# A hybrid pooling, spatial-gating and mLSTM layer: the gating projection in one pass of 512 columns, its weights split on VectorE, its rows normalised on ScalarE

## The chip, the cores and the metric

The kernel runs on one core of a Trainium2 chip. The metric is the device time of one execution in microseconds (us). The engines are named as the profile names them: PE is TensorE (PEld its weight loads), DVE is VectorE, ACT is ScalarE, POOL is GpSimd, SP is SyncE, which here only issues DMAs.

## The reference, cut to what matters

One layer works on 256 context tokens and 1024 latent tokens with the same weights. The part that the change touches is the input projection of the spatial branch's `v` half and the normalisation of its rows:

```python
u = rmsnorm(x, g_norm1) * (1 + sc1) + sh1
proj = u @ w_in
xp, su, sv, q, k, v, o_pre, gate_pre, br_pre = jnp.split(proj, points, axis=-1)
y_a = pool_branch(xp, w_pool, pool_scale, grid)
y_b = sgu_branch(su, sv, g_sgu, w_sgu, b_sgu)      # 512 columns each
y_c, C_out, n_out, m_out = mlstm_branch(q, k, v, o_pre, ...)

def sgu_branch(u, v, g_sgu, w_sgu, b_sgu):
    vn = rmsnorm(v, g_sgu).reshape(B, T // CHUNK, CHUNK, N_SGU_GROUPS, SGU_GROUP)
    mixed = jnp.einsum('gpq,bnqgc->bnpgc', w_sgu, vn) + ...
    return u * mixed.reshape(B, T, D_SGU)
```

All of it is float32. The three branches are gated, summed and projected (`w_out`), and a feed-forward follows with 4096 hidden columns.

## The kernel before, in words

The 1280 tokens are ten tiles of 128 (NT = 10), or three token groups of 512, 512 and 256 columns. The contraction over the model's 1024 features is eight steps of 128 (KT = 8). A float32 product is made of three matmuls on rounded halves: high by high, low by high and high by low. Weights arrive by DMA as `raw` tiles of 128x1024, two at a time (NRAW = 2). `load_w` (L88 to L95) makes the high half with a cast on ACT (L93) and the low half with a subtraction on an engine that the caller names (L94). There are three buffers for each half (NHL = 3). Activations and results live in 59 buffers of 128x512, called slots (L55), which are given out again once the last reader of a slot is done.

In PSUM there are three banks for large products (`ps_mm`) and five for smaller ones (`ps_sd`). A bank is free again when the last instruction that reads it is done.

The order of the instructions on each engine is not the order of the source, outside a pinned prologue. A scheduler that simulates the program puts the instructions of all engines into an order when the program is built; on the chip each engine takes its own row strictly in that order, and waits at the first instruction whose inputs or whose buffer are not ready. A change in one place can therefore move work elsewhere.

The part around the change runs from about 273 to 421 us. Two heads of the mLSTM branch (the third and the fourth, whose tiles carry the head's number 2 and 3) and the projections for them and for the pooling branch (`p_xp`) are interleaved with the `sv` matmuls, which are independent of the heads and fill PE between their steps. One head does the following. `tk` and `tv` transpose keys and values on PE (L582, L586); ACT copies them out (L583, L587), DVE scales them (L590). `kv` (L597) are 18 matmuls that DVE adds one after the other into a running state (L608, L613). `st` and `rb` (L626, L630) give the weights of a group, made ready on DVE and ACT (L634 to L644). `pv` (L659, L661) gives the outputs of a tile. From there a chain of small steps goes through ACT, DVE and POOL: L664, L665, L666, L667, L668, L669, L129, L130 (the power -0.5, on POOL) and L673 (rows scaled, on ACT); then `th` transposes the result on PE (L674) and ACT copies it out (L676, `yc`).

The `sv` part itself (L697 to L716) goes twice over the ten token tiles, each time with 256 of the 512 weight columns. Per tile it runs 24 matmuls of 256 columns into one bank (L707 to L709), ACT copies the bank to the slot `vn` (L710) and squares it with a sum over the row (L711). Each pass loads its own two weight tiles, the low halves on POOL. After the second pass the two sums of a row are added on DVE (L713), `rstd_of` makes the reciprocal root (L129 on DVE, L130 on POOL), and DVE scales the ten tiles (L716). The scaled rows are the stationary side of the `mx` matmuls in `spatial` (L840), whose results DVE takes (`mt`, L844) and multiplies with the projection `p_su` (L851). The pooling branch works beside it on DVE and POOL (L767).

Of the kernel before, what the change touches and what calls it, by code (L numbers as in the profile page):

```python
# [7 lines left out]
F32 = mybir.dt.float32  # L8
F32R = mybir.dt.float32r
AF = mybir.ActivationFunctionType  # L10
ALU = mybir.AluOpType
# [3 lines left out]
P = 128  # L15
D = 1024
KT = D // P
NSAMP = 1024
T = 1280
NT = T // P  # L20
# [8 lines left out]
NTMP, NRAW, NHL = 5, 2, 3  # L29
# [19 lines left out]
def hybrid_step(  # L49
# [8 lines left out]
    V, A, G, PE = engines  # L58
# [6 lines left out]
    wp = pw.enter_context(tc.tile_pool(name="wp", bufs=NRAW))  # L65
# [3 lines left out]
    def slot(name, dt=F32R):  # L69
        return sp.tile([P, 512], dt, tag="s", name=name)  # L70
# [4 lines left out]
    def ps_mm(name):  # L75
        return pp.tile([P, 512], F32, tag="mm", name=name, bufs=3)
# [4 lines left out]
    def small(shape, name, bufs=4):  # L81
        return cp.tile(shape, F32, tag=f"sm{shape[-1]}", name=name, bufs=bufs)
# [6 lines left out]
    def load_w(src, name, raw=None, eng=V):  # L89
        raw = fetch_w(src, name) if raw is None else raw  # L90
        hi = wp.tile([P, 1024], F32R, tag="hi", name=f"hi_{name}", bufs=NHL)
        lo = wp.tile([P, 1024], F32R, tag="lo", name=f"lo_{name}", bufs=NHL)
        A.copy(hi, raw)  # L93
        eng.tensor_tensor(lo, raw, hi.bitcast(F32), ALU.subtract)  # L94
        return hi, lo  # L95
# [125 lines left out]
    uT = [[] for _ in range(KT)]  # L221
# [54 lines left out]
    V, A, G, PE = (Pinned(tc, e) for e in engines)  # L276
# [119 lines left out]
    for at, (g, k) in enumerate(steps):  # L396
# [3 lines left out]
        if (g, k) == (1, 2):  # L400
# [4 lines left out]
            for i in range(2):  # L405
                w = slot(f"wgs{i}").rearrange("p (k c) -> p k c", c=P)
# [25 lines left out]
    V, A, G, PE = engines  # L432
# [84 lines left out]
    for g in range(3):  # L517
        t0, n = GROUPS[g]
        r = slot(f"rhl{g}")
# [173 lines left out]

    vn = []
    vsq = cp.tile([P, NT, 2], F32, name="vsq")
    for q in range(2):
        wq = [load_w(w_sv[q, hf], f"sv{q}_{hf}", eng=G) for hf in range(2)]  # L697
        for i in range(NT):
            g, o = (i * P) // 512, (i * P) % 512
            if q == 0:  # L700
                vn.append(slot(f"vn{i}", F32))
            ps = ps_mm(f"sv{q}_{i}")
            for k in range(KT):
                whi, wlo = wq[k // 4]
                s = slice((k % 4) * 256, (k % 4 + 1) * 256)
                uh, ul = uT[k][g]
                PE.matmul(ps[:, :256], uh[:, o : o + P], whi[:, s], start=k == 0, stop=False)  # L707
                PE.matmul(ps[:, :256], ul[:, o : o + P], whi[:, s], start=False, stop=False)
                PE.matmul(ps[:, :256], uh[:, o : o + P], wlo[:, s], start=False, stop=k == KT - 1)  # L709
            A.copy(vn[i][:, q * 256 : (q + 1) * 256], ps[:, :256])  # L710
            A.activation(ps[:, 256:512], ps[:, :256], AF.Square, accum_out=vsq[:, i, q : q + 1])  # L711
    vs1 = small([P, 16], "vs1")[:, :NT]
    V.reduce_sum(vs1, vsq, axis=mybir.AxisListType.X)  # L713
    r = rstd_of(vs1, NT, "v")
    for i in range(NT):
        V.tensor_scalar(vn[i], vn[i], r[:, i : i + 1], None, ALU.mult)  # L716

    def zs(i, n=1):
        return z[:, i * 512 : (i + n) * 512]
# [336 lines left out]
    for ri, r in enumerate(ORDER):  # L1056
        scr = (scr_ya, scr_yb, scr_yc)[r]
        ys = [[] for _ in range(4)]
        for g in range(3):
            for kc in range(4):  # L1060
                t0, n = GROUPS[g]
                raw = tmp2(f"yr{r}_{kc}_{g}")
# [407 lines left out]
def _layout(inputs):  # L1470
    import numpy as np

    f = {k: np.asarray(v) for k, v in inputs.items()}
    a = {}
    a["xs"] = np.concatenate([f["x_sample"][0], f["x_prompt"][0]], 0).reshape(NT, P, D)

    def col(v, n):
        return v.reshape(n, P).T

    cond = np.stack([f["c"][0], f["c_ctx"]], -1).reshape(KT, P, 2).transpose(1, 0, 2).reshape(P, 16)  # L1480
    a["cols"] = np.concatenate(
        [
            cond, col(f["b_ada"][0, :2048], 16), col(f["g_norm1"][0], 8), col(f["g_norm2"][0], 8),
            col(f["pool_scale"][0], 4), col(f["g_sgu"][0], 4), col(f["g_mlstm"][0], 4),
        ], 1)
    s = np.arange(P)
    neg = np.float32(-1e30)
    a["consts"] = np.concatenate(
        [
            np.eye(P, dtype=np.float32),  # L1490
            np.where(s[:, None] <= s[None, :], np.float32(0), neg),
            np.where(s[:, None] >= s[None, :], np.float32(0), neg),
            np.tile(np.eye(2, dtype=np.float32), (64, 1)),
        ], 1).astype(np.float32)
    sel = np.zeros((100, 8), np.float32)
    for d in range(2):
        for h in range(H):
            sel[32 * d + h, 4 * d + h] = 1.0
            sel[64 + 32 * d + h, 4 * d + h] = 1.0
    a["sel8"] = sel  # L1500
    a["w_ada"] = f["w_ada"][0]
    a["b_ada"] = f["b_ada"]
    w = f["w_in"][0]
    wd = np.concatenate([w[:, :1024], w[:, 1536:3584], w[:, 3600:]], 1)
    a["w_in"] = wd.reshape(KT, P, 48, P).transpose(2, 1, 0, 3).reshape(48, P, KT * P)
    a["w_sv"] = w[:, 1024:1536].reshape(2, 4, P, 2, 256).transpose(3, 0, 2, 1, 4).reshape(2, 2, P, 1024)
    wgt = np.zeros((KT, P, P), np.float32)
    wk = w[:, 3584:3600].reshape(KT, P, 16)
    bg = np.zeros((36, 2), np.float32)
    m0 = np.zeros((36, 1), np.float32)  # L1510
    for t in range(2):
        for d in range(2):
            j = t * 8 + d * 4
            for o in (0, 4):
                wgt[:, :, 64 * t + 32 * d + o : 64 * t + 32 * d + o + 4] = wk[:, :, j : j + 4]
            bg[32 * d : 32 * d + 4, t] = f["b_gates"][0, j : j + 4]
    for d in range(2):
        m0[32 * d : 32 * d + 4, 0] = f["state_m"][0, 0, d]
    a["w_gate"] = wgt.transpose(1, 0, 2)
    a["bg"], a["m0"] = bg, m0  # L1520
    a["w_branch"] = f["w_branch"][0].reshape(3, 4, P, 4, 256).transpose(0, 3, 2, 1, 4).reshape(3, 4, P, 1024)
    a["w_out"] = f["w_out"][0].reshape(KT, P, 2, 512).transpose(2, 0, 1, 3)
    a["w_ff1"] = f["w_ff1"][0].reshape(KT, P, NFF, P).transpose(2, 1, 0, 3).reshape(NFF, P, D)
    a["w_ff2"] = f["w_ff2"][0].reshape(NFF, P, D)
    a["w_pool"] = f["w_pool"][0].transpose(1, 0, 2)
    a["w_sgu"] = f["w_sgu"][0].transpose(2, 0, 1)
    a["b_sgu"] = f["b_sgu"][0].reshape(1, 4 * P)

    def inv(n, win):
        t = np.arange(n)  # L1530
        cnt = np.clip(t + win - win // 2, 0, n) - np.clip(t - win // 2, 0, n)
        return (np.float32(1.0) / cnt.astype(np.float32)).astype(np.float32)

    a["pcnt"] = np.stack([
        np.concatenate([np.outer(inv(GRID_H, w_), inv(GRID_W, w_)).ravel(), inv(256, w_)]) for w_ in POOL_WINDOWS])
    st = np.concatenate([f["state_C"][0, 0], f["state_n"][0, 0][..., None]], -1)
    a["state"] = st.transpose(1, 2, 0, 3)
    a["gfin"] = f["g_final"].reshape(1, D)
    return {k: np.ascontiguousarray(v) for k, v in a.items()}
# [31 lines left out]
```

## Time and profile before

| what | value |
|---|---|
| time, median of 3 runs (lowest, highest) | 1940.14 us (1939.9, 1941.92) |
| the profiled execution's own time | 1940.92 us |
| its span in the profile | 1939.1 us |
| mean granted PE clock | 0.996 |
| PE busy / DVE / ACT / POOL | 98% / 67% / 44% / 19% |
| first `sv` matmul, first `p_su` matmul | 273.31 us, 420.66 us |

The median belongs to the timed runs, the rows of the profile to one execution of its own, which took 0.78 us longer than the median. A matmul's duration in the rows includes its filling and draining, which the next one overlaps; the pace of PE is therefore the distance between the starts of successive rows. A number in brackets at a row's end is the idle time of the engine before that instruction, with what ended it.

### The profile page before, as it was taken

The page shows a single profiled execution, that of the slowest core. Times are in us where ns is not written, and L with a number is a line of the kernel's source. Part 1 is how long each engine was busy: PE and PEld are TensorE (multiplying, and loading weights), DVE is VectorE, ACT ScalarE, POOL GpSimd, SP SyncE. Part 2 cuts the span into 40 slices and gives each one's busy share as a digit, 9 for nine tenths or more (in the row PEclk, how much of TensorE's full clock was granted, in tenths as well). Part 3 has the DMA queues.
Part 4 walks back from the last instruction along what each step waited for, and adds up shares of the span by engine and source line. Part 5 has one row for each costly group of instructions (what it writes and reads, how often), then busy time and mean ns, then how long its engine had stood idle before and what let it go on. Part 6 is the DMA issues. An engine that isn't in the chain of part 4 may idle for free.

```text
span 1939.1 us, 28222 instructions
## 1 busy us (share of the span) xinstructions
PE 1904.2 (98%) x10142; PEld 1628.1 (84%) x10142; DVE 1306.1 (67%) x2234; ACT 848.7 (44%) x1771; POOL 376.6 (19%) x381
## 2 busy tenths in 40 slices
PE   8989999999999999999999999999999999999998
PEld 5878898988888888888888887888888888888886
DVE  6575435578597878876665598887776655744665
ACT  6444455532433333342113375554454544443343
POOL 1100011064032422220000015544431210000003
PEclk9999999999999999999999999999999999999999
DMA  9211111025353434469622435777774686655544
GB/s 367 80 60 32 46 39 39 33 82 201 126 181 131 148 131 156 143 222 341 198 77 100 162 109 214 267 256 269 255 248 141 202 323 201 213 170 151 158 140 160
DMA packets 152774, 318.56 MB, mean 164 GB/s; under 512 B 17934, under 2 KB 42226, under 8 KB 150586
## 3 DMA queue, kind: packets, MB, share of 16 engines
q1 hardware_dynamic: 109082, 223.35, 35.1%
q0 software_dynamic: 15520, 57.75, 8.0%
q10 hardware_dynamic: 28032, 35.67, 5.1%
q8 instruction: 79, 1.29, 0.3%
q14 instruction: 61, 0.50, 0.1%
HBM read 220.21 MB, written 95.98 MB: 163 GB/s over the span
## 4 chain that ended last, share of the span: by engine, by line
PE 86%; DVE 5%; DMA 4%; ACT 2%; POOL 2%; issue 1%; SPq 0%; POOLq 0%; ACTq 0%; DVEq 0%
PE w L1438 6%; PE w L1439 6%; PE w L1440 6%; PE pb L1086 3%; PE pb L1085 3%; PE pb L1087 3%; PE fT_g L921 3%; PE fT_g L919 3%; PE fT_g L920 3%; PE fT L919 3%; PE fT L920 3%; PE fT L921 3%; PE fB L921 2%; PE fB L920 2%; PE fB L919 2%; PE fB_g L921 2%
## 5 line engine op out<-in xcount | busy, mean ns | idle before, releaser
L1277 POOL TENSOR_TENSOR z<-z 128x512 f32<-128x512 f32 x64 | 100.6, 1571 | 120.7 <-DMA z<-in_w_ff 117.7
L547 POOL PARTITION_ALL_REDUCE acc<-acc x16 | 54.5, 3441 | 226.5 <-DVE acc L541 123.0
L976 DVE TENSOR_TENSOR z<-z 128x512 f32<-128x512 f32 x120 | 94.9, 791 | 2.7
L541 DVE SCALAR_TENSOR_TENSOR acc<-z,scond,acc 128x512 f32<-128x512 f32 x112 | 82.3, 781 | 0.0
L1392 POOL TENSOR_TENSOR rs_y<-rs_y,neghalf 128x1 f32<-128x1 f32 x10 | 9.6, 966 | 332.8 <-DVE rs_y L1391 332.8
L1243 ACT ACTIVATE z<-z 128x512 f32<-128x512 f32 x64 | 40.5, 632 | 70.6 <-DVE z L985 35.6
L1002 ACT ACTIVATE z<-z 128x512 f32<-128x512 f32 x56 | 35.4, 632 | 65.3 <-DVE z L985 17.7
L130 POOL TENSOR_TENSOR rs_h<-rs_h,neghalf 128x4 f32<-128x4 f32 (+1 forms) x12 | 10.9, 910 | 178.8 <-DVE rs_h L129 144.0
L1091 DVE TENSOR_TENSOR sg<-pb,sg 128x512 f32<-128x512 f32 (+1 forms) x48 | 28.7, 601 | 24.0 <-PE pb L1087 23.9
L1244 ACT ACTIVATE z<-z 128x512 f32<-128x512 f32 x64 | 40.3, 629 | 1.1
L910 ACT CAST hi_wb<-raw_wb 128x512 fp32r<-128x512 f32 x24 | 14.8, 620 | 57.2 <-PE pb L1086 44.6
L1206 DVE TENSOR_TENSOR po<-po,gt 128x512 f32<-128x512 f32 (+1 forms) x24 | 14.6, 609 | 35.4 <-PE po L1205 35.3
L767 POOL TENSOR_TENSOR z<-z 128x256 f32<-128x256 f32 (+13 forms) x20 | 34.7, 1745 | 13.7 <-ACT z L752 5.5
L1268 POOL DMA_DIRECT2D scr_s<-x x48 | 26.3, 548 | 52.9 <-DVE x L1262 47.2
L548 POOL TENSOR_TENSOR acc<-acc,bt 1x512 f32<-1x512 f32 x16 | 22.3, 1408 | 60.0 <-issue 60.0
L1209 ACT ACTIVATE po<-z 128x512 f32<-128x512 f32 (+1 forms) x24 | 12.7, 529 | 48.3 <-DVE z L1208 34.0
L608 DVE SCALAR_TENSOR_TENSOR z<-z,dmb,kv 128x129 f32<-128x129 f32 x56 | 17.0, 346 | 22.1 <-PE kv L597 21.6
L665 DVE TENSOR_TENSOR den<-den,gcol 128x2 f32<-128x2 f32 x40 | 6.2, 165 | 38.0 <-ACT den L664 37.8
L634 DVE SCALAR_TENSOR_TENSOR w<-rb,gcol,cst 128x128 f32<-128x128 f32 x48 | 13.3, 343 | 24.5 <-PE rb L630 24.5
L1092 DVE TENSOR_TENSOR z<-z,sg 128x512 f32<-128x512 f32 (+1 forms) x48 | 28.6, 600 | 1.1
L590 DVE TENSOR_TENSOR z<-tv,gcol 128x512 f32<-128x512 f32 (+1 forms) x24 | 14.2, 601 | 17.5 <-ACT z L587 17.3
L130 POOL TENSOR_TENSOR rs_f<-rs_f,neghalf 128x4 f32<-128x4 f32 (+1 forms) x3 | 3.3, 1091 | 116.9 <-DVE rs_f L129 116.9
(5360 smaller groups left out, 7293.3 us busy)
## 6 DMA issues: line engine op xcount, KB each, us to landing
z<-in_w_ff SPq DMA_DIRECT2D x64, 512.0 KB, 5.3
z<-in_w_ada SPq DMA_DIRECT2D x64, 256.0 KB, 3.0
scr_t<-z POOLq DMA_DIRECT2D x16, 1024.0 KB, 4.4
z<-in_w_in SPq DMA_DIRECT2D x28, 512.0 KB, 4.3
scr_g<-z ACTq DMA_DIRECT2D x48, 256.0 KB, 2.0
sg<-scr_g SPq DMA_DIRECT2D x48, 256.0 KB, 4.5
scr_h<-z ACTq DMA_DIRECT2D x48, 256.0 KB, 3.3
scr_s<-x POOLq DMA_DIRECT2D x48, 256.0 KB, 3.9
```

Source lines behind the costliest of these rows:

```text
L541: V.scalar_tensor_tensor(acc[j], raw, scond[:, k, j : j + 1], acc[j], ALU.mult, ALU.add)
L919: PE.matmul(ps, whi[:, s], ahi, start=first and k == ks[0], stop=False)
L920: PE.matmul(ps, whi[:, s], alo, start=False, stop=False)
L921: PE.matmul(ps, wlo[:, s], ahi, start=False, stop=end and k == ks[-1])
L976: V.tensor_tensor(out, x, y, op)
L1085: PE.matmul(pb[:, :n], whi[:, s], yh, start=kc == 0, stop=False)
L1086: PE.matmul(pb[:, :n], whi[:, s], yl, start=False, stop=False)
L1087: PE.matmul(pb[:, :n], wlo[:, s], yh, start=False, stop=kc == 3)
L1277: G.tensor_tensor(out, x, y, ALU.subtract)
L1438: PE.matmul(banks[j], h_[:, s], rh, start=fp == 0, stop=False)
L1439: PE.matmul(banks[j], l_[:, s], rh, start=False, stop=False)
L1440: PE.matmul(banks[j], h_[:, s], rl, start=False, stop=fp == NFP - 1)
```

## The change

The `sv` weights are laid out as four tiles of 128x1024, each with two of the eight contraction steps and all 512 columns. They are fetched once. Each half tile of 512 columns is cast on ACT and subtracted on DVE, no more on POOL. Three of the four weight tiles use the buffers of `load_w`; the fourth has four slots (`hi_sv30`, `lo_sv30`, `hi_sv31`, `lo_sv31`). One pass over the ten token tiles follows, with 24 matmuls of 512 columns for each tile and one copy and one square of 512 columns. There is one sum per row, so the addition on DVE goes, and the ten rows of tiles are scaled by ACT.

```diff
@@ -693,27 +693,36 @@
     vn = []
     vsq = cp.tile([P, NT, 2], F32, name="vsq")
-    for q in range(2):
-        wq = [load_w(w_sv[q, hf], f"sv{q}_{hf}", eng=G) for hf in range(2)]
-        for i in range(NT):
-            g, o = (i * P) // 512, (i * P) % 512
-            if q == 0:
-                vn.append(slot(f"vn{i}", F32))
-            ps = ps_mm(f"sv{q}_{i}")
-            for k in range(KT):
-                whi, wlo = wq[k // 4]
-                s = slice((k % 4) * 256, (k % 4 + 1) * 256)
-                uh, ul = uT[k][g]
-                PE.matmul(ps[:, :256], uh[:, o : o + P], whi[:, s], start=k == 0, stop=False)
-                PE.matmul(ps[:, :256], ul[:, o : o + P], whi[:, s], start=False, stop=False)
-                PE.matmul(ps[:, :256], uh[:, o : o + P], wlo[:, s], start=False, stop=k == KT - 1)
-            A.copy(vn[i][:, q * 256 : (q + 1) * 256], ps[:, :256])
-            A.activation(ps[:, 256:512], ps[:, :256], AF.Square, accum_out=vsq[:, i, q : q + 1])
-    vs1 = small([P, 16], "vs1")[:, :NT]
-    V.reduce_sum(vs1, vsq, axis=mybir.AxisListType.X)
+    vs1 = vsq[:, :, 0]
+    wsv = []
+    for j in range(4):
+        raw = fetch_w(w_sv[j], f"sv{j}")
+        for kk in range(2):
+            rk = raw[:, kk * 512 : kk * 512 + 512]
+            if j < 3:
+                if kk == 0:
+                    whole = [wp.tile([P, 1024], F32R, tag=t, name=f"{t}_sv{j}", bufs=NHL) for t in ("hi", "lo")]
+                hi, lo = (t[:, kk * 512 : kk * 512 + 512] for t in whole)
+            else:
+                hi, lo = slot(f"hi_sv{j}{kk}"), slot(f"lo_sv{j}{kk}")
+            A.copy(hi, rk)
+            V.tensor_tensor(lo, rk, hi.bitcast(F32), ALU.subtract)
+            wsv.append((hi, lo))
+    for i in range(NT):
+        g, o = (i * P) // 512, (i * P) % 512
+        vn.append(slot(f"vn{i}", F32))
+        ps = ps_mm(f"sv{i}")
+        for k in range(KT):
+            whi, wlo = wsv[k]
+            uh, ul = uT[k][g]
+            PE.matmul(ps, uh[:, o : o + P], whi, start=k == 0, stop=False)
+            PE.matmul(ps, ul[:, o : o + P], whi, start=False, stop=False)
+            PE.matmul(ps, uh[:, o : o + P], wlo, start=False, stop=k == KT - 1)
+        A.copy(vn[i], ps)
+        A.activation(ps, ps, AF.Square, accum_out=vs1[:, i : i + 1])
     r = rstd_of(vs1, NT, "v")
     for i in range(NT):
-        V.tensor_scalar(vn[i], vn[i], r[:, i : i + 1], None, ALU.mult)
+        A.activation(vn[i], vn[i], AF.Copy, scale=r[:, i : i + 1])
...
-    a["w_sv"] = w[:, 1024:1536].reshape(2, 4, P, 2, 256).transpose(3, 0, 2, 1, 4).reshape(2, 2, P, 1024)
+    a["w_sv"] = w[:, 1024:1536].reshape(4, 2, P, 512).transpose(0, 2, 1, 3).reshape(4, P, 1024)
```

Lines after the scaling move down by nine: `mx` goes from L840 to L849, `mt` from L844 to L853. In the changed kernel the `sv` matmuls are L718 to L720, the copy and the square L721 and L722, the scaling L725, the cast and the subtraction of the weights L708 and L709.

The order on the engines before the first `sv` matmul stays as it was. Three places behind it are shown; in all of them a name like `sv_3438` is one bank's product for one token tile.

**The state chain of the third head on PE.** Before, `sv` matmuls stand between the `kv` matmuls that DVE adds up one by one (`sv_4_3528` is the fifth tile of the first pass):

```order
L709 MATMUL sv_4_3528<-lo_sv_1_3412,u4h_809 128x256
L597 MATMUL kv_7_1_2490<-z 128x129
L597 MATMUL kv_1_0_2493<-z 128x129
L597 MATMUL kv_6_1_2496<-z 128x129
L707 MATMUL sv_4_3528<-hi_sv_1_3411,u5h_827 128x256
L708 MATMUL sv_4_3528<-hi_sv_1_3411,u5l_828 128x256
L597 MATMUL kv_2_0_2499<-z 128x129
L597 MATMUL kv_5_1_2502<-z 128x129
L709 MATMUL sv_4_3528<-lo_sv_1_3412,u5h_827 128x256
```

In the changed kernel (`sv_3438`, `sv_3466` and `sv_3494` are the first three token tiles, in the three banks at once; `u7` is the last contraction step, whose weights are in the slots):

```order
L719 MATMUL sv_3494<-hi_sv_3433,u7l_635 128x512
L597 MATMUL kv_7_1_2490<-z 128x129
L597 MATMUL kv_1_0_2493<-z 128x129
L597 MATMUL kv_6_1_2496<-z 128x129
L597 MATMUL kv_2_0_2499<-z 128x129
...
L597 MATMUL kv_9_1_2536<-z 128x129
L597 MATMUL kv_8_1_2539<-z 128x129
L626 MATMUL st_0_2544<-qT_0_2389,kT_0_2216 128x128 x4
...
L720 MATMUL sv_3438<-lo_sv_3434,u7h_634 128x512
```

Of the 18 `kv` matmuls 17 now follow each other, 11 of them left out above, and the three `sv` tiles are finished only after them.

**The end of the third head on PE.** Before, behind the last `pv` and ahead of `th_2` (the transposes of the head's last group):

```order
L661 MATMUL pv_9_2771<-z,e_2_2683 128x129
L659 MATMUL pv_9_2771<-z,w_2_1_2689 128x129
L707 MATMUL sv_2_3761<-hi_sv_0_3697,u0h_384 128x256
...
L709 MATMUL sv_3_3788<-lo_sv_1_3704,u6h_610 128x256
L674 MATMUL th_2_2785<-cst,z 128x128
L582 MATMUL tk_0_3053<-cst,kT_0_2825 128x128 x2
```

In the changed kernel at the same place:

```order
L661 MATMUL pv_9_2771<-z,e_2_2683 128x129
L659 MATMUL pv_9_2771<-z,w_2_1_2689 128x129
L674 MATMUL th_1_2748<-cst,z 128x128 x3
L674 MATMUL th_2_2785<-cst,z 128x128
L582 MATMUL tk_0_3053<-cst,kT_0_2825 128x128 x4
L586 MATMUL tv_0_3059<-cst,vT_0_2911 128x128 x4
...
L718 MATMUL sv_3634<-hi_sv_3405,u0h_706 128x512
```

Before, 45 `sv` matmuls stood between; now only three transposes do, and the next `sv` tile, the eighth, comes behind the transposes of the fourth head.

**The spatial mixing on PE.** Before, `mx` stood directly behind the last `p_xp` matmul and ahead of the first `p_su` one. In the changed kernel:

```order
L125 MATMUL p_xp_3995<-u7c,lo_xp_3938 128x256
L123 MATMUL p_su_4072<-u0h_384,hi_su_4068 128x512
...
L125 MATMUL p_su_4072<-u7h_634,lo_su_4069 128x512
L123 MATMUL p_su_4099<-u0h_706,hi_su_4068 128x512
L849 MATMUL mx_0_4047<-z,vn_3437 128x128
```

The 24 matmuls of the first `p_su` product now stand ahead of `mx`.

## Prediction

> **What bounds the kernel now.** I read the page first, then windows, then PE's waits. The first row of the page and the head of the chain that ended last:
>
> ```profile
> PE 1904.2 (98%) x10142; PEld 1628.1 (84%) x10142; DVE 1306.1 (67%) x2234; ACT 848.7 (44%) x1771; POOL 376.6 (19%) x381
> PE 86%; DVE 5%; DMA 4%; ACT 2%; POOL 2%; issue 1%; SPq 0%; POOLq 0%; ACTq 0%; DVEq 0%
> ```
>
> PE is busy for 1904.2 of 1939.1 us. A change gains only by what it takes from PE's own work, or from the 35 us in which PE is idle, and the whole kernel is PE's row in its order. So I ask what PE does and waits for between 273.31, where `sv` begins, and 420.66, where `p_su` begins. The windows of that stretch in which something happens (columns: window, length, then busy time and count of PE, PEld, DVE, ACT, POOL, granted clock, DMA share, GB/s):
>
> ```profile
> 280.00:290.00 10.00, 9.67 (x83) 9.43 (x82) 3.83 (x9) 5.66 (x19) 0.70 (x1) 1.00 0.14 52
> 290.00:300.00 10.00, 10.00 (x88) 10.00 (x88) 5.00 (x18) 0.54 (x2) 0.00 (x0) 1.00 0.00 0
> 310.00:320.00 10.00, 8.68 (x74) 8.47 (x74) 4.59 (x15) 6.75 (x24) 3.38 (x2) 1.00 0.00 0
> 320.00:330.00 10.00, 8.15 (x66) 7.52 (x65) 5.08 (x22) 7.81 (x33) 1.01 (x1) 1.00 0.44 140
> 330.00:340.00 10.00, 9.15 (x77) 8.95 (x77) 1.43 (x7) 4.29 (x17) 0.70 (x1) 1.00 0.08 28
> 400.00:420.00 20.00, 20.00 (x128) 18.02 (x127) 16.30 (x21) 9.17 (x22) 15.27 (x14) 1.00 0.29 86
> ```
>
> PE stands still for about 4.35 us here, all of it between 280 and 340. The waits of PE from 260 to 380, and from 380 to 600 (in total, times, longest):
>
> ```profile
> PE sv L707 <- ACT sv L711: 2.2, 4, 0.8
> PE th L674 <- ACT z L673: 1.3, 1, 1.3
> PE pv L659 <- ACT yc L676: 0.8, 1, 0.8
> ...
> PE mx L840 <- ACT ya L794: 1.2, 1, 1.2
> PE pp L792 <- PE p_su L125: 0.5, 1, 0.5
> PE fB_g L921 <- DVE a_g0l L902: 0.4, 1, 0.4
> ```
>
> Four `sv` tiles waited for a bank (the release is the square L711), one `th` for the scaled rows, one `pv` for the copy `yc`. That is 4.3 us, so PE's own work in the stretch is some 143 us of 147.35.
>
> **The change on PE.** The pace of 256-column and of 512-column matmuls, by the first and the last row of a run of each:
>
> ```profile
> 278.80 0.28 PE L708 MATMUL sv<-hi_sv,u2l 128*128 128x256 f32 x1
> 280.96 0.28 PE L708 MATMUL sv<-hi_sv,u0l 128*128 128x256 f32 x1
> ...
> 263.18 0.39 PE L124 MATMUL p_q<-u1l,hi_q 128*128 128x512 f32 x1
> 266.15 0.40 PE L125 MATMUL p_q<-u5h,lo_q 128*128 128x512 f32 x1
> ```
>
> 18 steps in 2.16 us are 0.120 us each; 13 steps in 2.97 us are 0.2285 each. 480 matmuls take 57.6 us, 240 of twice the width 54.8: **-2.8 us**. These rows show that number of columns and not the number of instructions sets most of the cost: halving the instructions saves 5%.
>
> The Trainium skill, "TensorE: Matmul & The Clock Gate", section "Back-to-back issue gap", would give less: it has a gap of N/2.4 + 2.5 ns, 216 against 109 ns, so two narrow matmuls cost only some 2.5 ns more than a wide one, and by an estimate from it the term is -0.6 us instead of -2.8. Both figures lie below this trace's 228.5 and 120 ns. The rows are taken from this kernel with these types, so the sum goes by them.
>
> Returning from the heads' float32 matmuls to the split ones costs something too:
>
> ```profile
> 291.61 0.83 PE L597 MATMUL kv<-z 128*128 128x129 f32 x6
> 292.20 0.36 PE L707 MATMUL sv<-hi_sv,u5h 128*128 128x256 f32 x1
> 292.40 0.28 PE L708 MATMUL sv<-hi_sv,u5l 128*128 128x256 f32 x1
> ```
>
> The first `sv` matmul behind `kv` holds PE for 0.20 instead of 0.12 us. Between 273 and 421 us the order has 43 such returns before and 31 after, since the heads' matmuls now stand in longer runs: 12 x 0.08 = **-1.0 us**.
>
> **The waits that replace the old ones.** The old 4.3 us hang on the old order. The new order has its own places, each priced by rows.
>
> First, the state chain of the third head. DVE's part of it, and the release of a bank in the old kernel:
>
> ```profile
> 292.03 1.52 DVE L608 SCALAR_TENSOR_TENSOR z<-z,dmb,kv 128x129 f32<-128x129 f32 x5 [1.79 <-PE kv L597]
> ...
> 327.65 0.28 PE L709 MATMUL sv<-lo_sv,u7h 128*128 128x256 f32 x1
> 327.96 0.37 ACT L710 COPY vn<-sv 128x256 f32<-128x256 f32 x1 [0.78 <-PE sv L709]
> 328.23 0.38 ACT L711 ACTIVATE sv<-sv 128x256 f32<-128x256 f32 x1
> 328.54 0.19 ACT L711 ACTIVATION_READ_ACCUMULATOR sv<-sv 128x1 f32 x1
> 328.77 0.39 PE L707 MATMUL sv<-hi_sv,u0h 128*128 128x256 f32 x1 [0.85 <-ACT sv L711]
> ...
> L349 ACT ACTIVATE qT<-p_q x7: 598/599/622, 98.6 to 270.6; 128x512 f32<-128x512 f32 x7
> ```
>
> One state update is 0.303 us (1.52 / 5); one `kv` on PE, two rows, is 0.222 (0.56 / 5 x 2). While `sv` matmuls stood between, PE never noticed: 10.00 of 10 us busy from 290 to 300. Now 17 stand alone: 14 updates take 4.25 us, PE's 17 take 3.8, so it waits 0.45 for the banks of `ps_sd`, and perhaps 0.25 before it for the scaled values (L590). Why the `sv` work cannot fill this: the last weight piece sits in slots that come free only as the head's old ones are read, so three tiles in three banks wait open for `u7`. When they close at last, the fourth needs the first one's bank. The release took 1.12 us from the last matmul's start to the next (328.77 - 327.65); with 512 columns the copy and the square are each some 0.22 longer (0.60 against 0.38), so 1.56, less the two other tiles' last matmuls, 0.46: 1.1. Together **+1.8 us**, bounded by 0 (another engine's row is earlier than I think) and 3.
>
> Second, `pv` behind `yc` remains at about **+0.3** (0.8 before), and the seventh tile's bank is late, between 0 and 1.56: I take **+0.9**, since its copy stands on ACT between the steps of the head's tail.
>
> Third, the end of the third head. The chain from the last `pv` to `th` in the old kernel, where it happened to be undisturbed:
>
> ```profile
> 277.27 0.39 PE L659 MATMUL pv<-z,w 128*128 128x129 f32 x2
> 280.39 0.70 POOL L130 TENSOR_TENSOR rs_h<-rs_h,neghalf 128x2 f32<-128x2 f32 x1 [2.87 <-DVE rs_h L129]
> 281.12 0.70 ACT L673 ACTIVATE z<-z,rs_h 128x128 f32<-128x128 f32 x2 [1.08 <-POOL rs_h L130]
> 318.61 0.33 PE L674 MATMUL th<-cst,z 128*128 128x128 f32 x1 [1.32 <-ACT z L673]
> ```
>
> Last `pv` matmul at 277.38, L673 at 281.12, and `th` can follow its L673 in 0.46: 4.2 us. In the old order 45 `sv` matmuls, 5.4 us, covered it. Now only three transposes do, 0.33, and PE takes its row in order, so `th_2` waits 3.7 us and the fourth head's `tk` and `tv` and the eighth tile stand behind it. Then ACT must copy `tk` and `tv` before it closes the fifth tile, so the eighth's bank is another 0.8 late (two copies of 0.6, partly beside PE's transposes). **+4.5 us**, bounded by 2 and 6. The one wait of this kind that the old kernel had, 1.3 us, goes away, because 24 wide matmuls, 5.5 us, now lie between.
>
> Sum of new waits: 1.8 + 0.3 + 0.9 + 4.5 = 7.5, against 4.3 gone: **+3.2 us**.
>
> **ACT, DVE and POOL.** The removed row scaling on DVE looks like the large gain. The chain that ends at 425 has it in its middle:
>
> ```profile
> 407.35 10.08 DVE vn L716 x7
> 417.43 0.08 issue
> 417.51 1.27 DVE vn L716 x3
> ...
> 418.39 0.28 PE L125 MATMUL p_xp<-u7c,lo_xp 128*128 128x256 f32 x1
> 418.51 2.40 PE L840 MATMUL mx<-z,vn 128*128 128x128 f32 x20
> ```
>
> But `mx` starts 0.12 us behind the last `p_xp` matmul, one normal step, and PE was busy for 20.00 of 20 us: 11.4 us of DVE were hidden, just in time. So their removal is worth **0** here. On ACT the ten scalings cost at most 10 x 0.60 = 6 us; ACT was busy for 9.17 of these 20 us. They stand behind L673 of the last head and one copy. From the last `pv` that is 3.7 us to L673 (281.12 - 277.38), 0.7 for it, 0.6 for the copy and 6.0 for the scalings, 11.0 us in all, while PE has 13.9 us of `th`, `p_xp` and `p_su` work up to `mx` (its instructions counted in the order, at the paces above), the 24 matmuls that moved ahead included. If the new place were not there, these 5.5 us would be missing and `mx` would wait 2.6 us. The weight halves (DVE, 8 of some 0.6 us) lie in a stretch where DVE is busy half the time, and the four subtractions leave POOL, which was idle most of the time: 0.
>
> From 421 us on the 0.5 us before `pp` L792 should go, since DVE is 11 us freer, while the 1.2 us before `mx` may come back larger: **-0.2**, with bounds of -2 (all three waits quoted above go) and +3.
>
> **The sum.** -2.8 - 1.0 + 3.2 - 0.2 = -0.8 us. The profiled execution took 1940.92 us (span 1939.1), so the profiled time after would be 1940.1. The median of the runs shown is 0.78 below the profiled one, 1940.14; minus 0.8 that gives **1939.4 us**.
>
> **Rivals.**
>
> *The waits do not come.* If the scheduler's order fits the chip, the old 4.3 us go and nothing takes their place: -2.8 - 1.0 - 4.3 - 0.2 = -8.3, 1931.8 us. For it speaks that ACT is busy less than 80% in every window above. Against it, the tail chain's 4.2 us is measured and no work stands in front of it. Chance 0.17.
>
> *The banks become the limit: slower.* Place: the three banks of `ps_mm`. A tile's bank returns 1.56 us after its last matmul where ACT is free, and later where copies of the heads (0.60 each) or casts stand ahead on ACT. Seven tiles reuse a bank; the forecast lets three wait. If all seven wait for one copy and the release, 7 x (1.56 + 0.6) = 15.1 instead of the 2.8 counted, so up to +12; if the other four wait for the release alone, 4 x 1.56 = +6.2. It decides from the point where ACT closes a tile later than PE's 5.5 us for the next one. For it: four of the old tiles waited already, with shorter evictions. Against: the old 20 evictions become 10. Time about 1939.4 + 6.6 = 1946 us. Chance 0.17.
>
> *The scaling on DVE was on the path after all*, as the chain has it: 11.4 us come out, less nothing else, about 1928. Against it stands the 20.00. Chance 0.05.
>
> *Two narrow matmuls cost hardly more than a wide one.* Were the 512-column pace of `sv` 0.238 us instead of the 0.2285 of `p_q`, as much as two narrow ones less 2 ns, 2.2 us of the gain would go, 1941.6. For it speaks no row, only that no wide `sv` matmul has run yet. Chance 0.08. The Trainium skill's rule in the section named above has the same consequence, a term of -0.6.
>
> **How the numbers follow.** The forecast has 0.53, with a range of its own from 1936.5 to 1942.8. A measurement of this kernel can tell 0.2%, 3.9 us, from no change, so faster is below 1936.3 and slower above 1944.0. Faster: 0.17 + 0.05 + 0.02 of the forecast's edge = 0.24. Slower: 0.17 + 0.02 = 0.19. Within: 0.57. The range from 1931.5 to 1946.0 leaves out the DVE case, the lower 0.07 of the first rival and the upper half of the second, 0.20 in all.
>
> **What would show it.** Right: 512-column `sv` steps of 0.2285 us; one PE wait of 3 to 4 us at `th` behind L673 near 340 us with `tk` after it; a gap of about a microsecond behind the third head's `kv` run; no wait at the first `mx`. The stretch from the first `sv` to the first `p_su` minus `mx` shrinks by about 0.6 us. Wrong: waits of more than 2 us in total at `sv` tiles four to ten outside these places (the banks), a wait at `mx` behind L725, or a `kv` run and a `th` without a gap (then the first rival). A `th` wait above 6 us would mean that ACT or POOL is late in the chain itself.

## The result and the profile after

| | before | after |
|---|---|---|
| median of 8 runs (lowest, highest) | 1939.53 us (1938.51, 1943.58) | 1946.25 us (1942.82, 1949.39) |
| ratio to before, 95% interval | | 1.0029 (1.0019 to 1.0038) |
| profiled execution (span) | 1940.92 us (1939.1) | 1942.82 us (1941.0) |
| first `sv` matmul / last `mx` matmul in the profile | 273.3 / 493.5 us | 270.9 / 494.5 us |

The change makes the kernel slower by 0.29%, some 5.6 us (the ratio goes by the means of the runs; the medians lie 6.7 apart). The forecast was a gain of 0.8 us. The profiled execution of the changed kernel is the fastest of its eight runs, so its profile shows less than the usual loss. One more caution: the first `sv` matmul begins 2.4 us earlier here, though everything ahead of it on PE stands in the same order. In the profiles of this study it began anywhere between 270.4 and 273.8 us. I therefore compare the part from the first `sv` to the last `mx`: 220.2 us before, 223.6 after, and 221.6 in a second profile of the changed kernel (e1 below).

The first row of the page and three rows of the windows (window, length, busy time and count of PE, PEld, DVE, ACT, POOL, granted clock, DMA share, GB/s) of the changed kernel:

```profile
PE 1905.5 (98%) x9902; PEld 1618.2 (83%) x9902; DVE 1289.5 (66%) x2231; ACT 853.4 (44%) x1755; POOL 369.8 (19%) x377
...
330.00:340.00 10.00, 6.04 (x45) 5.24 (x44) 2.83 (x9) 6.46 (x21) 0.70 (x1) 1.00 0.07 26
400.00:420.00 20.00, 20.00 (x110) 17.32 (x109) 3.48 (x9) 13.61 (x33) 16.45 (x16) 1.00 0.24 80
460.00:480.00 20.00, 15.36 (x77) 11.78 (x76) 18.43 (x27) 6.50 (x11) 3.77 (x3) 0.95 0.85 274
```

Two holes stand out: 4 us between 330 and 340, 4.6 us between 460 and 480. In the second one the granted clock is below 1 too. Between them, from 400 to 420, DVE does 3.48 us of work instead of 16.30, and it gains nothing: PE was full there before and is full now. What PE waited for, from 260 to 380 and from 380 to 600:

```profile
PE th L674 <- ACT z L673: 3.3, 1, 3.3
PE sv L718 <- ACT sv L722: 1.9, 3, 0.8
...
PE mx L849 <- ACT ya L803: 4.6, 2, 2.6
PE fB_g L930 <- DVE a_g0l L911: 0.4, 1, 0.4
```

The first hole is the wait that the prediction had placed, at `th` behind the last `pv`. PE's timeline (start, duration, instruction, and in brackets the idle time before it):

```profile
332.57 0.49 PE L674 MATMUL th<-cst,z 128*128 128x128 f32 x3
336.40 0.33 PE L674 MATMUL th<-cst,z 128*128 128x128 f32 x1 [3.34 <-ACT z L673]
336.56 0.60 PE L582 MATMUL tk<-cst,kT 128*128 128x128 f32 x4
```

The second is the third block of `mx` matmuls. The same timeline there, before, with rows of ACT:

```profile
474.75 1.95 PE L840 MATMUL mx<-z,vn 128*128 128x128 f32 x16
477.85 0.71 PE L840 MATMUL mx<-z,vn 128*128 128x128 f32 x4 [1.16 <-ACT ya L794]
...
469.20 0.62 ACT L818 CAST T4h<-z 128x512 fp32r<-128x512 f32 x1 [0.23 <-DVE z L809]
...
477.11 0.69 ACT L794 ACTIVATE ya<-pp,ccol 128x512 f32<-128x512 f32 x1 [2.94 <-DMA scr_yb<-mt]
```

And after, with rows of ACT and one of DVE:

```profile
472.58 2.05 PE L849 MATMUL mx<-z,vn 128*128 128x128 f32 x16 [2.01 <-ACT ya L803]
477.27 0.71 PE L849 MATMUL mx<-z,vn 128*128 128x128 f32 x4 [2.64 <-ACT ya L803]
...
478.43 0.63 PE L124 MATMUL p_su<-u5l,hi_su 128*128 128x512 f32 x1
478.85 0.63 PE L125 MATMUL p_su<-u5h,lo_su 128*128 128x512 f32 x1
...
481.69 0.39 PE L123 MATMUL p_su<-u0h,hi_su 128*128 128x512 f32 x1
481.92 0.39 PE L124 MATMUL p_su<-u0l,hi_su 128*128 128x512 f32 x1
...
463.94 0.69 ACT L803 ACTIVATE ya<-pp,ccol 128x512 f32<-128x512 f32 x1 [1.84 <-PE pp L801]
471.32 0.62 ACT L827 CAST T4h<-z 128x512 fp32r<-128x512 f32 x1 [6.69 <-DVE z L818]
471.85 1.05 ACT L803 ACTIVATE ya<-pp,ccol 128x512 f32<-128x512 f32 x2
...
476.53 1.27 ACT L803 ACTIVATE ya<-pp,ccol 128x512 f32<-128x512 f32 x2 [1.57 <-DMA scr_yb<-mt]
...
469.99 1.89 DVE L818 TENSOR_TENSOR z<-z 128x512 f32<-128x512 f32 x3 [1.02 <-DMA z<-scr_u]
```

`mx` needs a bank of `ps_sd` that `ya` still has to copy out. The first wait, 2.01 us, is new: its `ya` stands on ACT behind a cast (L827) that waits 6.69 us for the sums on DVE (L818), and these wait for a load; before, that cast waited 0.23 us. The second wait, 2.64 us against 1.16 before, ends in both kernels with a store: its `ya` (477.11 before, 476.53 now) takes one of the five `tmp` buffers (NTMP = 5), which it shares with the `mt` tiles, and waits until a store of `mt` has left it. PE arrived at this block at 474.75 before and at 470.6 now. Counted from the first `sv` that is 201.4 and 199.7 us, so PE comes 1.7 us sooner, while the last four `mx` start 1.9 us later (206.4 against 204.5). PE came early to a place that another chain sets, this chain ends later in the new order, and the wait is 4.6 us instead of 1.2. Behind the wait there is something else to see: the `p_su` matmuls start 0.42 us apart (478.43, 478.85) and only from 481.69 on 0.23 again. In windows of 2 us:

```profile
478.00:480.00 2.00, 2.00 (x6) 1.59 (x6) 1.97 (x4) 0.99 (x2) 0.00 (x0) 0.52 0.84 293
480.00:482.00 2.00, 2.00 (x7) 1.54 (x7) 2.00 (x4) 0.00 (x0) 0.00 (x0) 0.63 0.78 301
482.00:484.00 2.00, 2.00 (x11) 1.62 (x10) 1.14 (x3) 0.00 (x0) 0.00 (x0) 1.00 0.03 9
```

The granted clock falls to half for more than 3 us behind the idle time: 0.48 x 2 + 0.37 x 2 = 1.7 us lost. PE counts as fully busy there, so no busy share shows it; only the clock's column and the pace do.

### The profile page after: what moved, and what is told of

Read it like the earlier page. It is cut to its first block, busy times and chain, and to the rows that moved or that the text cites. A ratio compares the mean times of both kernels' runs of the same rounds, so it can differ in the third digit from the quotient of the medians.

```text
span 1941.0 us, 27718 instructions
## 1 busy us (share of the span) xinstructions
PE 1905.5 (98%) x9902; PEld 1618.2 (83%) x9902; DVE 1289.5 (66%) x2231; ACT 853.4 (44%) x1755; POOL 369.8 (19%) x377
## 4 chain that ended last, share of the span: by engine, by line
PE 90%; DVE 4%; DMA 3%; ACT 2%; issue 1%; POOL 0%; SPq 0%; POOLq 0%; ACTq 0%; DVEq 0%
PE w L1447 6%; PE w L1448 6%; PE w L1449 6%; PE fT L930 3%; PE fT L928 3%; PE fT L929 3%; PE pb L1094 3%; PE pb L1095 3%; PE pb L1096 3%; PE fT_g L928 3%; PE fT_g L930 3%; PE fT_g L929 3%; PE fB L929 2%; PE fB L930 2%; PE fB L928 2%; PE fB_g L930 2%
## 5 line engine op out<-in xcount | busy, mean ns | idle before, releaser
L985 DVE TENSOR_TENSOR z<-z 128x512 f32<-128x512 f32 x120 | 95.0, 791 | 2.7
L994 DVE TENSOR_TENSOR z<-z 128x512 f32<-128x512 f32 x30 | 26.3, 877 | 0.0
```

The lines of the kernel that those rows point to most:

```text
L985: V.tensor_tensor(out, x, y, op)
```

## The experiments

The theories: **A**, PE's gain turns into idle time at the third `mx` block, and the clock falls behind it. **B**, the waits of the new order up to 340 us are the loss. **C**, the ten scalings as one block on ACT are. **D**, the pooling stage begins late because the last head ends late. **K**, long waits let the granted clock fall, in some runs and not in others. All ratios are to the kernel before on the same chip, with 95% intervals; 0.1% is 1.9 us.

**e1: the changed kernel again.**

> The changed kernel unchanged, for a second profile. Theory A (the pooling stage on VectorE and POOL sets when the last mx matmuls run, about 477 us, so TensorE's gains before it turn into idle time, and after that idle time the granted clock falls): again 4 us or more of TensorE idle between 470 and 478 us, a clock near 0.5 for 3 to 4 us behind it, time 1943 to 1949. Theory B (the waits of the new order between 290 and 340 us are the loss): idle time there above 8 us, and no clock loss.

Median 1945.95 us (1943.05 to 1948.53, 7 runs), ratio 1.0031 (1.0020 to 1.0041). The profiled execution was the fastest again, 1943.05. Idle: 3.3 us at `th`, 4.1 at `mx`. But its clock did not fall, neither near 340 nor near 478 us; its mean over the execution is 0.997. So theory A's fall is not there each time. Both profiles of this kernel without a fall near 340 us belong to the fastest of their seven or eight runs, which suggested K.

**e2: the scaling back on VectorE.**

```diff
-        A.activation(vn[i], vn[i], AF.Copy, scale=r[:, i : i + 1])
+        V.tensor_scalar(vn[i], vn[i], r[:, i : i + 1], None, ALU.mult)
```

> The changed kernel with only the row scaling put back on VectorE; TensorE's order is the same but for four places near 437 us. Theory C (the ten scalings as one block on ScalarE delay the copies that feed the pooling stage): 1 to 4 us faster than the changed kernel. Theory A: VectorE was idle for 10 us at this place, so about the same, at most 3 us slower because the scalings run beside POOL and the next weight half waits for them.

1946.41 us, ratio 1.0033 (1.0023 to 1.0044): no gain. For C this is a weak test, because the edit makes a wait of its own: the first `mx` block now waits for the scaling on DVE, and the clock falls behind it (0.50 from 430 to 436 us).

```profile
PE mx L849 <- DVE vn L725: 3.4, 2, 1.8
PE mx L849 <- ACT ya L803: 1.7, 1, 1.7
```

This profile is of a slower run, 1948.74 us, and shows what the two others lacked. Its windows behind the same 3.34 us wait at `th`, and below them those of e1:

```profile
336.00:338.00 2.00, 0.00 (x0) 0.00 (x0) 0.41 (x2) 0.79 (x5) 0.69 (x1) 0.75 0.34 131
338.00:340.00 2.00, 1.79 (x9) 1.79 (x10) 0.00 (x0) 0.88 (x3) 0.00 (x0) 0.50 0.00 0
340.00:342.00 2.00, 2.00 (x11) 2.00 (x10) 0.92 (x2) 1.73 (x6) 0.00 (x0) 0.50 0.00 0
342.00:344.00 2.00, 2.00 (x8) 1.71 (x7) 1.34 (x3) 2.00 (x6) 0.00 (x0) 0.54 0.03 8
```

```profile
334.00:336.00 2.00, 0.00 (x0) 0.00 (x0) 0.41 (x2) 0.79 (x5) 0.69 (x1) 1.00 0.34 131
336.00:338.00 2.00, 1.78 (x16) 1.79 (x17) 0.00 (x0) 1.44 (x5) 0.00 (x0) 1.00 0.00 0
338.00:340.00 2.00, 1.39 (x9) 1.05 (x8) 1.39 (x2) 2.00 (x7) 0.00 (x0) 1.00 0.00 0
```

The wait is equally long to the hundredth of a microsecond in both. In one execution the clock falls during it and stays at half for some 6 us; in the other it does not. One pair of executions suggests K and does not show it.

**e3 and e4: the two small parts alone**, in the kernel before, with PE's order exactly as it was. e3 makes e2's edit the other way round, e4 changes `eng=G` to `eng=V` in `load_w` of the `sv` weights.

> The kernel before with only the row scaling moved to ScalarE; TensorE's order is exactly the same as before. Theory C: 1 to 3 us slower. Theory A: VectorE starts its pooling work about 1 us earlier, so the 1.2 us wait before the last mx shrinks: 0 to 1.5 us faster.

> The kernel before with only the four low halves of the spatial weights made on VectorE instead of POOL; TensorE's order is exactly the same. All theories: within 1 us of before, since neither engine is late there. A loss of 2 us or more would mean that the weights' split itself is the cost of the change.

e3: 1938.28 us, 0.9995 (0.9985 to 1.0004). e4: 1939.83 us, 0.9995 (0.9986 to 1.0005). Neither costs anything, so C falls, for the two-pass order at least. In both the wait before the third `mx` block shrinks, from 1.16 to 0.31 us (e3) and 0.55 us (e4). The loss must come from the single pass and the order that the scheduler makes around it.

**e5: the last head ends earlier.**

```diff
-    pool_project(1)
+    with tc.issue_after(last_pv[0].ins):   # last pv matmul of the last head
+        pool_project(1)
```

> The changed kernel with one thing ordered otherwise: the p_xp matmuls of the third pooling group stand behind the last head's last pv on TensorE, not ahead of it. Theory D (the pooling stage on POOL and VectorE may only begin when the last pv has read the shared workspace z; the changed order puts some 8.8 us more p_xp work ahead of that pv, so the stage ends late and ya and mx with it): the first POOL memset behind pv some 5.5 us earlier, the wait at the third mx block down from 4.6 us to at most 1.2, no clock fall behind it, 3 to 5 us faster than the changed kernel, so within 2 us of before. Theory B (the wait at th near 336 us is the loss): the same time as the changed kernel within 1 us.

1946.92 us (5 runs), 1.0037 (1.0023 to 1.0050): no gain. PE's waits:

```profile
PE th L675 <- ACT z L674: 4.9, 2, 3.3
PE mx L850 <- ACT ya L804: 3.0, 1, 3.0
PE sv L719 <- ACT sv L723: 1.5, 3, 0.8
```

The wait at `mx` shrank from 4.6 to 3.0, and a new one of 1.6 came at the last head's `th`. As a way to mend the loss, D falls; B did not predict the shorter wait at `mx`, but the same time. The clock fell behind both long waits in this profile (0.50 at 336 to 338 and 0.50 at 480 to 482 us).

**e6: matmuls that nobody reads, in the wait at `th`.** They go to the unused half of `th`'s own bank. Their time falls into the wait.

```diff
             ps = ps_sd(f"th{h}_{g}")
+            if h == 2 and g == 2:
+                ua = uT[0][0][0]
+                for _ in range(FILL):      # FILL = 26
+                    tc.keep_in_program_order(PE.matmul(ps[:, 256:512], ua[:, 0:P], ua[:, 0:256], start=True, stop=True))
```

> The changed kernel with 26 matmuls of 256 columns, whose results nobody reads, put into TensorE's row just where it waits for th of the third head; the order is otherwise the same. The wait lasts as long, but TensorE runs through it. Theory K (long waits let the granted clock fall in some runs, about 3 us each time): the wait at th shrinks from 3.3 to about 0.3 us without the next work starting earlier, no low clock near 340 us, the fastest runs unchanged at 1943 and the median 1 to 2.5 us lower than the changed kernel. If only the length of the wait counts: the same median within 1 us.

1941.96 us (1940.17 to 1943.48, 11 runs), 1.0006 (0.9997 to 1.0015). From the first `sv` to the last `mx` it took 221.5 us, as e1 did, so nothing starts earlier; no fall near 340 us. Some 4 us are gone from the median though PE does more work. Unlike what I expected, the fastest runs fell too, by 2.6 us. I had not foreseen that the next head's `tk` and `tv` would move ahead of `th` in this order, which left a doubt that e13 settles.

**e7: e5 and e6 together.**

> The changed kernel with both: the p_xp work behind the last pv, and the 26 matmuls in the wait at th. If D and K hold and add up: 4 to 7 us faster than the changed kernel, between 1939 and 1942 us, with all runs within 4 us of each other. It still has the 3.3 us wait at th, so it should not be clearly faster than before.

1942.75 us, 1.0013 (1.0004 to 1.0022): 0.24% below e5, the same step as from e1 to e6, in another order. e5's part adds nothing, and the 4 to 7 us expected did not come. At the third `mx` block PE waits 1.95 us here, and the clock falls behind it (0.50 from 478 to 480 us).

**e8: the wait put into the kernel before.**

```diff
+                with tc.issue_after(last_th[2, 2].ins) if (q, i) >= (1, 2) else nullcontext():
                     PE.matmul(ps[:, :256], uh[:, o : o + P], whi[:, s], start=k == 0, stop=False)
...
```

> The kernel before with only this changed: the sv matmuls of the second pass from the third tile on stand behind the third head's th, so that nothing covers the chain from pv to th, as in the changed kernel. By moving them it also brings the last head forward by some 5 us. Theory B (the uncovered th is the loss): a wait of 3 to 4 us at th and 3 to 5 us slower than before, with a clock fall near 340 us in some runs. Theory D: the wait at th is there, but the pooling stage starts 5 us earlier and the wait before mx goes away, so only 0 to 3 us slower.

1941.81 us, 1.0009 (1.0000 to 1.0018). The waits, and the windows behind `th`:

```profile
PE th L675 <- ACT z L674: 5.1, 2, 3.7
PE sv L709 <- ACT sv L713: 1.4, 3, 0.8
PE pv L660 <- ACT yc L677: 0.8, 1, 0.8
```

```profile
338.00:340.00 2.00, 2.00 (x15) 2.00 (x16) 0.19 (x1) 1.44 (x5) 0.00 (x0) 0.74 0.00 0
340.00:342.00 2.00, 2.00 (x11) 2.00 (x10) 1.73 (x3) 2.00 (x9) 0.00 (x0) 0.50 0.00 0
342.00:344.00 2.00, 2.00 (x18) 2.00 (x18) 0.85 (x2) 0.83 (x3) 0.00 (x0) 0.90 0.19 66
```

A wait of 3.75 us made in the old kernel brings the fall along: 0.26 x 2 + 0.50 x 2 + 0.10 x 2 = 1.7 us. No wait at `mx` is left: PE reaches the third block 3.6 us later than in the kernel before (205.1 against 201.4 us after the first `sv`), so this delay takes the old wait's place, and only 1.7 us are lost. B alone doesn't make the loss.

**e9: both small parts, still two passes.**

> The kernel before with both small parts of the change, the row scaling on ScalarE and the low weight halves on VectorE, but still two passes of 256 columns; TensorE's order is exactly as before. If the single pass with its order is the whole loss: 0 to 2 us faster than before. If the two parts cost something together that neither costs alone: slower than before.

1939.26 us, 0.9990 (0.9980 to 1.0000). As expected: the single pass with its order is the whole loss. Neither the wait at `pp` nor the one at the third `mx` block is left here.

**e10: half as many unread matmuls.**

> The changed kernel with 13 instead of 26 unread matmuls in the wait at th: some 1.8 us of idle time are left there. Theory K (the clock falls only where TensorE is idle for about 3 us or more within a few microseconds): as fast as with 26, 1941 to 1943 us, and no low clock near 340 us. If any idle time costs in proportion: half of the gain, about 1944 us.

1943.41 us, 1.0012 (1.0002 to 1.0023). Inconclusive: with 13 of them the scheduler made another order. There was no wait at `th` at all, and the part up to the last `mx` took 216.3 us, the shortest of all; but later, at 1204 us, PE waited 3.7 us with a fall behind it, which the others don't, and 2.5 us at 1606 (none there in the changed kernel, 0.9 in e6, 1.7 in e13).

**e11: e6, and the third `mx` block behind the work that it held up.** `spatial` writes that block's matmuls behind the `p_su` matmuls of their token group.

```diff
-        mix = []
-        for g in range(3):
+        mix = [None] * 3
+        def mixed(g):
...
+        if ci not in LATE:                  # LATE = (2,)
+            for g in range(3):
+                mixed(g)
         def ev_su(g, ps):
+            if ci in LATE:
+                mixed(g)
```

> The changed kernel with the 26 matmuls and, beside them, the third block of mx matmuls written behind the p_su work of its token group instead of ahead of it, so that TensorE has work while ya is late. Theory K and the late pooling stage: the 4.6 us wait at mx is gone or below 1 us, no clock fall near 478 us, 3 to 5 us faster than with the filled th alone: 1937 to 1940 us. If the pooling stage bounds what follows anyway, the wait turns up at the next mx or pp: within 1 us of the filled th alone.

1937.12 us (1934.77 to 1938.87, 11 runs), 0.9979 (0.9971 to 0.9988). PE's waits from 262 to 520:

```profile
PE sv L724 <- ACT sv L728: 1.8, 3, 0.8
PE fB_g L943 <- DVE a_g0l L924: 0.4, 1, 0.4
```

The wait at `mx` is gone and does not come back elsewhere. That is 0.27% less than e6, some 5 us, for the 4.6 us of idle time that e6 has there. No fall followed that wait in e6's profile.

**e12: the same late block in two passes, with the two small parts.**

> The kernel before with ScalarE's row scaling, VectorE's weight halves and the late third mx block, in two passes: the version that these readings recommend. The wait of 1.2 us before mx goes, and it has no uncovered th: 1 to 3 us faster than before, 1937 to 1939 us; same as before within 0.1% if that wait was already gone with the scaling on ScalarE.

1938.96 us, 0.9988 (0.9979 to 0.9997): hardly below e9, whose wait at `mx` was already gone. The late block helps where PE comes early.

**e13: the unread matmuls, with the order held** (`tk` and `tv` behind `th`, as in the changed kernel).

```diff
+                with tc.issue_after(first_th[0].ins) if h == 3 else nullcontext():
                     PE.transpose(ps[:, c * P : (c + 1) * P], kT[g][:, c * P : (c + 1) * P], ident)
```

> The changed kernel with 26 unread matmuls in the wait at th and with the order held as it was: th of the third head ahead of the next head's tk and tv. Theory K (the clock falls after such a wait in most runs): as e6, 1941 to 1943 us, 3 to 5 us faster than the changed kernel. If the moved tk and tv carried the gain: 1945 to 1947 us, as the changed kernel.

1942.96 us (1941.50 to 1945.14, 11 runs), 1.0013 (1.0004 to 1.0021). Its waits:

```profile
PE mx L858 <- ACT ya L812: 4.4, 2, 2.4
PE sv L727 <- ACT sv L731: 1.9, 3, 0.8
...
PE th L681 <- ACT z L680: 0.3, 1, 0.3
```

The order is the changed kernel's, PE reaches every later place as late as there (220.2 + 3.4 = 223.6 us from `sv` to `mx`, with a fall at 478 in both), and still the median is 3 us lower. The moved `tk` and `tv` were not it. The changed kernel twice gave 1.0029 and 1.0031, the filled one 1.0006 and 1.0013: 0.20% between the means, with an interval of about 0.09% either way.

**e14: real work in the wait instead.** The last transposes of the third head are written behind the next head's `tk` and `tv`.

```diff
+            if h == 2 and g == 2:
+                turns.append(turn)          # th, yc and the store, as a function
+            else:
+                turn()
...
+            if g == 1 and turns:            # in head(): behind tk and tv
+                turns.pop()()
```

> The changed kernel with the last transposes (th, yc) of the third head written behind tk and tv of the next head's second group; nothing unread runs. TensorE has tk, tv and one sv tile, 7 us of work, between pv and th. The wait at th is gone, with it the clock fall: 3 us of idle time and about 3 us of slow clock, so 5 to 8 us faster than the changed kernel, 1938 to 1941 us. If the pooling stage swallows the idle time won: 1941 to 1943 us, as with the filled wait.

1942.56 us, 1.0013 (1.0004 to 1.0022): 3.3 us of idle time less at `th`, less gain than expected, and no better than e13, where PE spent the same time on unread matmuls. The waits now:

```profile
PE mx L860 <- ACT ya L814: 4.9, 2, 3.3
PE sv L729 <- ACT sv L733: 3.0, 3, 1.7
```

Of the 3.3 us, 1.1 went to the bank of an `sv` tile. PE reaches the third `mx` block 2.6 us sooner than in e13 (197.3 against 199.9 us after the first `sv`) and starts its last four only 0.7 us sooner (205.7 against 206.3): the rest is lost at `mx`, as the second expectation had it. Behind the longer wait there the clock falls (0.50 from 472 to 474 us).

**e15: e14 with the late third `mx` block.**

> e14 with the third mx block behind its group's p_su work as in e11. Nothing but the single pass's gain should be left: neither wait, no clock fall near 340 or 478 us, 1934 to 1938 us, faster than before by 3 to 6 us. If e11 gained by the filler and not by the cover: as e11 or slower.

1935.71 us (1933.03 to 1938.41, 11 runs), 0.9976 (0.9967 to 0.9985):

```profile
PE sv L730 <- ACT sv L734: 3.0, 3, 1.7
PE mx L862 <- ACT ya L815: 1.4, 1, 1.4
```

No fall between 140 and 1140 us. This version, the change with two places reordered, beats both kernels: by 0.24% the one before and by some 0.5% the changed one.

## Why the prediction was wrong

**PE's own work was right.** Over all `sv` rows the distances between starts add up to 60.6 us before and 56.8 after, -3.8 with the returns from float32 matmuls; the prediction's two terms make -3.8 together. The pace was 0.229 us (0.2285 forecast), so the lower gain by the issue gap did not come.

**The waits up to 340 us were right in place, and somewhat too high.** At `th` 3.34 us (3.7 forecast), at the banks 0.81, 0.45 and 0.61 (1.1, 0.9 and 0.8), at `pv` none (0.3). The `kv` run took 0.85 us more of PE's time (0.7). In all 5.2 us of idle time against 4.3 before. The stretch from the first `sv` to the first `p_su`, less `mx`, shrank by 1.2 us (0.6 forecast). Up to here the forecast was right.

**Scaling, weights and the first `mx` were right.** The scalings took 6.25 us on ACT (a little over the "at most" 6 us), and nothing waited for them. The chain's 11.4 us on DVE were no gain, as the 20.00 of PE had said: in two passes DVE's freed time was worth at most some 2 us, the waits at `pp` and `mx` that are gone in e9. With the single pass it does count, since the scaling on DVE makes PE wait 3.4 us (e2).

**The step that failed is "From 421 us on ... -0.2".** The 0.5 us before `pp` went, as forecast. For the wait of 1.2 us before `mx` the step said that it may come back larger; the -0.2 has only some 0.3 us for that, the bound +3, and no row stands behind either. It became 4.6 us (4.1 in e1), so in place of -0.2 the step measured +2.4 to +3.0 us. What was missing is the chain that ends this wait: loads, sums on DVE, the stores of `mt`, and `ya` on ACT. Any wait there, however short, says that PE has no slack against it. PE's gain of 1.7 us up to this block became idle time, and the chain itself ends later in the new order: in e6, whose first `sv` stands at the same 273.31 us as before, the last four `mx` start at 479.16 us against 477.85. Less work on DVE does shorten this wait, but only in the two-pass order (0.3 us in e3, none in e9). e14 and e15 show that PE's own gains do not count there: of the 2.6 us by which e14 reaches the block sooner than e13, 0.7 were left behind it, and only with the block out of the way is the time below the kernel before.

**A term was missing: the fall of the granted clock.** The sum counted a wait by its length. At `th` the wait comes with a fall that costs 1.4 to 2.8 us where a profile has it (e5, e2), and filling it took 0.20% off, about 4 us with an interval of some 2. At `mx` it cost 1.7 in the profile after, and a second fall in that profile, near 1180 us, as much again. The granted clock is on record for every timed run, as a mean over its span: the 118 runs of the kernel before have 0.9955, the 15 of the changed kernel (with e1) 0.9937, the 22 with the filled wait (e6, e13) 0.9955 again. That is 0.0018 of 1941 us, by an estimate that counts idle time too 3.5 us of clock, with an interval of 1.4 either way, and the filled wait gives it back. The profile before shows such falls as well, behind 3.04 us of idle time:

```profile
1150.00:1160.00 10.00, 6.88 (x45) 6.34 (x45) 7.62 (x22) 8.27 (x17) 1.90 (x2) 0.83 0.44 158
```

I read the clock only where the change is, and it was 1.00 in every quoted row. The Trainium skill has the rule, in "TensorE: Matmul & The Clock Gate", section "What's actually happening": the clock halves after an idle window of about 3.4 us, and the window runs freely, so where it lies differs from run to run. The trace agrees with the half (0.50) and with the chance: equal waits of 3.34 us with and without a fall. It agrees with the length of the window too, since half clock lasts 3.4 us or two or three times that. It doesn't agree that the idle time must reach 3.4 us: falls came behind waits of 2.98 us (e5) and 1.95 us (e7). This rule spoke against the change: by it an uncovered wait of 3.7 us is dearer than one of 1.3 by more than the difference.

Of the rivals, the banks were named for the slower side and did not come: three tiles waited, 1.9 us. The time lies where that rival put it, 1946 us (by 6.6 us, where its own terms give 6.2 or 12), for another reason: this is luck.

**What adds up.** Free of falls, the changed kernel's part up to `mx` is 1.4 to 1.7 us longer than before (221.6 to 221.9 against 220.2), and the filled versions are 0.6 to 1.3 thousandths slower, 1.2 to 2.5 us. The other 3 to 4 of the 5.6 us are the 3.5 us of clock that the changed kernel's runs lack on average. **Open** stays at which of the waits these falls stood: the one at `th` alone costs 1.4 to 2.8 by the rows, e14 has work there and still a mean clock of 0.9940, with its fall at `mx`, and e15, with the `mx` block moved as well, has 0.9955. In a single execution other things vary as much: the profiles of the changed kernel and of e1 took the same time, though the first lost 3.4 us more to falls. Open is also why the chain through the loads, DVE, the stores and `ya` ends later in the new order. In it the last head's last `pv` comes 7.6 us later after the first `sv` (135.7 against 128.1), but e5 brought that 3.5 us forward and gained nothing.

## What to carry to other kernels

When a change makes a stage faster, look for the next place at which its engine already waits, however shortly: the length of that wait says that there is no slack left, and the gain will arrive there as idle time unless work is moved in front. Price an uncovered wait of TensorE of 2 us or more at its length and, by chance, a clock fall behind it (1.3 to 3.0 us behind the waits between 300 and 500 us here), and put work into it (real if possible, unread if not). A single profile that is faster than the usual run may lack the very cause; compare it with the spread of the runs, read the mean granted clock of all of them, or take a second profile.

## What the runs showed of the hardware

- The granted clock falls to 0.50 behind TensorE's waits and comes back. Summed over windows of 2 us, the clock missing from one fall between 100 and 1900 us is 1.7 us, 3.4 or 5.1 in all 17 profiles, so half clock lasts 3.4 us or two or three times that.
- The length of the wait doesn't decide alone. Waits of 3.34 us in the same place gave a fall in two profiles (e2, e5) and not in two others (the changed kernel, e1); 3.75 us gave it in e8. The wait of 3.0 us before the transposes `pt` (near 1150 us) has a fall in all 17. Two waits of 2.0 and 2.6 us with 2 us of small matmuls between them gave it in the profile after and not in e6, and one of 1.95 us gave it in e7. Waits of 1.3 us and less were never followed by one up to 500 us; near 1180 us one came behind waits of 0.9 and 0.7 us (the changed kernel, e2; not e1).
- Matmuls whose results nobody reads, put into the wait at `th`, made the changed kernel faster by 0.17%, some 3 us, with the order of TensorE's other instructions held (e13).
- One scaling of 128x512 on ACT takes 0.71 us in the rows, ten in a row 6.25.
